# Half of an MLP's second matmul by seven block products instead of eight, with weight sums made by accumulating DMA

## The chip, the cores and the metric

One core of one Trainium2 chip runs the whole program. The metric is the device time of one execution in microseconds (us); lower is better. Five engines work side by side, each with its own in-order queue: TensorE (PE, its weight loads as PEld), VectorE (DVE), ScalarE (ACT), GpSimd (POOL) and SyncE (SP). SP, ACT and POOL also start DMA transfers.

## The reference, cut to what matters

The program is one decoder layer on 256 tokens of width 2048 (three token mixers, their merge, an output projection), then a squared-ReLU MLP and a last norm. The change lies in the last two lines, with `w_mlp_in` 2048 x 8192 and `w_mlp_out` 8192 x 2048, all in float32:

```python
h = h + mixed @ w_out[l]
u = rmsnorm(h, ln2_w[l])
h = h + jnp.square(jax.nn.relu(u @ w_mlp_in[l])) @ w_mlp_out[l]
return rmsnorm(h, lnf_w)[:, CHUNK:]
```

## The kernel before, in words

All weights lie in DRAM as **pieces** of 128 x 1024 float32 (512 KB): eight 128 x 128 blocks along the contraction, for 128 output channels. `weights` (L219) loads a piece into a `raw` buffer by a DMA from SP (L228), then `split` (L200) makes two float32r tiles of it: ACT casts it to `wh` (L201) and DVE subtracts to get the rest, `wl` (L202). So a product of float32 accuracy is made from float32r matmuls: high x high, high x low and low x high.

`product2` (L249) makes one output tile, 128 channels x 256 tokens with a contraction of 2048, from two pieces. The weights are the stationary operand. For each of 16 blocks there is one matmul with `wh` over 512 moving columns (the 256 tokens' high part beside their low part, L257) and one with `wl` over 256 columns (the high part alone, L259).

The MLP runs in four quarters `qd` of the hidden width. A quarter has 16 *mi* tiles (first matmul; ReLU, square and split into `hx`, L1290 to L1298) and then 16 *mo* tiles (second matmul over that quarter's 2048 hidden channels, summed over the quarters in `macc`, L1299 to L1318). Each tile takes two pieces, 256 pieces in all.

What sets the order: the kernel is written as a plain sequence, and a scheduler at build time lays it out on the queues by priority. Loads and splits of pieces are marked `tc.high_priority()`, so that they go as far ahead as their buffers let them. Those buffers are three `wh`, three `wl`, and the `raw` buffers of two pools: `more_raw` holds `(wp, 3)` and, from L1279 on, `(wp2, 3)`, and a counter `n_raw`, raised by one for each piece, sends odd numbers to `wp2` and even numbers to `wp`. A `raw` buffer is free again when both halves of its split are done. The partial sums of *trunk* products lie in three PSUM buffers (`trunk_psum`), others in five (`mx`).

```python
n_raw[0] += 1
rpool, bufs = more_raw[n_raw[0] % len(more_raw)]
raw = rpool.tile([P, 8, P], F32, tag="raw", bufs=bufs, name=uname("raw"))
nc.sync.dma_start(raw, a["w"][first + k])
```

Of the kernel before, what the change touches and what calls it, by code (L numbers as in the profile page):

```python
# [10 lines left out]
F32 = mybir.dt.float32  # L11
# [139 lines left out]
def tile_hybrid(ctx: ExitStack, tc: tile.TileContext, a, out, dbg=None):  # L151
# [23 lines left out]
    def V(k, j=0, n=1, rows=slice(0, P)):  # L175
        return vecs[rows, VCOL[k] + j:VCOL[k] + j + n]
# [13 lines left out]
    def uname(s):  # L190
        cnt[0] += 1
        return f"{s}_{cnt[0]}"
# [26 lines left out]
    def weights(key, ahead=True):  # L219

        first, n = PIECE[key]
        parts = []
        for k in range(n):
            with tc.high_priority() if ahead else ExitStack():
                n_raw[0] += 1
                rpool, bufs = more_raw[n_raw[0] % len(more_raw)]
                raw = rpool.tile([P, 8, P], F32, tag="raw", bufs=bufs, name=uname("raw"))
                nc.sync.dma_start(raw, a["w"][first + k])  # L228
                wh = wp.tile([P, 8, P], F32R, tag="wh", bufs=3, name=uname("wh"))
                wl = wp.tile([P, 8, P], F32R, tag="wl", bufs=3, name=uname("wl"))  # L230
                split(wh, wl, raw)
            parts.append((wh, wl))
        return parts

    def product(key, hi, lo, tok, kts=KT, ahead=True):

        n = tok.stop - tok.start
        ps = trunk_psum(n)
        last = kts // 8 - 1
        for k, (wh, wl) in enumerate(weights(key, ahead)):  # L240
# [8 lines left out]
    def product2(key, x):  # L249
# [11 lines left out]
        return full[:, :NR], full[:, NR:]  # L261

    def sigmoid(dst, src, nbias=0.0, sign=1.0):

# [980 lines left out]
    st_e = ExitStack()  # L1245
    ep = pool(st_e, "ep")
    wp2 = pool(st_e, "wp2")
    h1 = ep.tile([P, 16, NR], F32, name="h1")
    z2 = ep.tile([P, 2, 16, NR], F32R, name="z2")
    acc2 = ep.tile([P, NR], F32, name="acc2")  # L1250
    r2 = ep.tile([P, NR], F32, name="r2")
    macc = ep.tile([P, 16, NR], F32, name="macc")
# [9 lines left out]
    def add_square(c, src):  # L1262
        s = et("sqe")
        act.activation(s, src, AF.Square)
        if c == 0:
            vec.tensor_copy(acc2, s)
        else:
            vec.tensor_tensor(acc2, acc2, s, add)

    for c in range(16):  # L1270
        xr = et("xr", 3)
        nc.scalar.dma_start(xr, a["xt"][:, c, NM:])
        ps, lo = product2(("out", c), m2)
        vec.tensor_tensor(h1[:, c], lo, xr, add)
        vec.tensor_tensor(h1[:, c], ps, h1[:, c], add)
        z = et("z")
        act.activation(z, h1[:, c], AF.Copy, scale=V("ln2", c))
        split(z2[:, 0, c], z2[:, 1, c], z)
        add_square(c, h1[:, c])  # L1279
# [6 lines left out]
    act.activation(r2, r2, AF.Exp, scale=-1.0)  # L1286
    st_y = ExitStack()
    yp = pool(st_y, "yp", side="right")
    for qd in range(4):
        hx = yp.tile([P, 2, 16, NR], F32R, tag="hx", bufs=2, name=uname("hx"))  # L1290
        for c in range(16):
            ps, lo = product2(("mi", 16 * qd + c), z2)
            vec.tensor_tensor(ps, ps, low_part(lo), add)
            r = et("rl")
            act.activation(r, ps, AF.Relu)
# [3 lines left out]
        for c in range(16):  # L1299
            ps, lo = product2(("mo", qd, c), hx)  # L1300
            if qd == 0:
                act.copy(macc[:, c], ps)
            elif qd < 3:
                vec.tensor_tensor(macc[:, c], ps, macc[:, c], add)
            if qd < 3:
                vec.tensor_tensor(macc[:, c], lo, macc[:, c], add)
            else:
                vec.tensor_tensor(ps, ps, low_part(lo), add)
            if qd == 2:
                vec.tensor_tensor(macc[:, c], macc[:, c], r2, mult)  # L1310
                vec.tensor_tensor(h1[:, c], h1[:, c], macc[:, c], add)
            if qd == 3:
                t = et("rs")
                vec.tensor_tensor(t, ps, r2, mult)
                vec.tensor_tensor(h1[:, c], h1[:, c], t, add)
                if c < 15:
                    add_square(c, h1[:, c])
                    act.activation(h1[:, c], h1[:, c], AF.Copy, scale=V("lnf", c))  # L1318
    pn = mx()[:, :NR]
    pe.matmul(pn, lhsT=C("ones"), rhs=acc2, start=True, stop=False)  # L1320
    s = et("sqe")
# [7 lines left out]
    act.activation(rp_, rl, AF.Exp, scale=-0.5)  # L1329
    act.activation(rf, rl, AF.Exp, scale=-0.5)  # L1330
    for k, (lo, hi) in enumerate(((0, 2), (2, 5), (5, 8), (8, 11), (11, 13))):
        vec.tensor_tensor(macc[:, lo:hi], h1[:, lo:hi],
                          rp_.unsqueeze(1).to_broadcast([P, hi - lo, NR]), mult)
        (nc.scalar if k % 2 else nc.sync).dma_start(out[:, lo:hi], macc[:, lo:hi])
    for c in range(13, 16):
        nc.gpsimd.tensor_tensor(macc[:, c], h1[:, c], rf, mult)  # L1336
    nc.scalar.dma_start(out[:, 13:16], macc[:, 13:16])
    st_y.close()
    st_e.close()

# [95 lines left out]
```

## Time and profile before

| | us |
|---|---|
| median of three runs (lowest, highest) | 1904.9 (1904.66, 1906.49) |
| the profiled execution | 1904.59 |
| its span in the trace | 1902.8 |
| PE busy | 1881.6 |
| DVE busy | 1288.1 |
| ACT busy | 1071.3 |
| POOL busy | 189.7 |

The span is the stretch that the trace covers; about 1.8 us of the profiled execution lie around it. A busy share is a mean over the span, so what a stage costs is read from that stage. The granted clock of TensorE has two levels, 1.2 and 2.4 GHz; a value of 1.00 is the upper one.

### The profile page before, as it was taken

Reading aid. Unit: us, or ns where it says so; the run is one execution under the profiler, and the core shown is the slowest. Engines: PE = TensorE matmul, PEld = TensorE weight load, DVE = VectorE, ACT = ScalarE, POOL = GpSimd, SP = SyncE. Lnnn points to the kernel's source line nnn. Section 1 sums busy time; section 2 is a strip of 40 time slices with the busy share of each in tenths; the row PEclk is TensorE's granted clock in tenths of the full one; section 3 lists DMA queues with packets and bytes.
Section 4 is the critical chain, followed back from the end, with each engine's and each line's share of the span. In section 5 each row is a group of like instructions: output and inputs, shape, how many; then the busy total and the mean of one; then the engine's idle time right before and its main releaser. Section 6 shows DMA issues by size and latency. Waiting matters only on the chain.

```text
span 1902.8 us, 35349 instructions
## 1 busy us (share of the span) xinstructions
PE 1881.6 (99%) x13910; PEld 1745.0 (92%) x13910; DVE 1288.1 (68%) x2126; ACT 1071.3 (56%) x1943; POOL 189.7 (10%) x317
## 2 busy tenths in 40 slices
PE   8999999999999999999999999999999999999997
PEld 8999999999999999999999988888888888888886
DVE  7878677668956667677677776654566556775575
ACT  7666566656556667676564455544454345435554
POOL 5110111112111111112121000000000000000000
PEclk9999999999999999999999999999999999999998
DMA  7556544444554445444657775556555555555562
GB/s 248 177 188 197 162 147 156 131 155 163 185 156 155 151 150 194 146 153 161 207 170 220 246 222 194 187 184 187 186 188 187 188 188 187 186 189 183 186 189 99
DMA packets 104103, 340.12 MB, mean 179 GB/s; under 512 B 18216, under 2 KB 21432, under 8 KB 103936
## 3 DMA queue, kind: packets, MB, share of 16 engines
q1 hardware_dynamic: 92480, 316.79, 51.8%
q0 software_dynamic: 8576, 17.67, 3.0%
q10 hardware_dynamic: 2880, 3.39, 0.5%
q8 instruction: 109, 1.79, 0.4%
q14 instruction: 58, 0.48, 0.1%
HBM read 327.72 MB, written 10.08 MB: 178 GB/s over the span
## 4 chain that ended last, share of the span: by engine, by line
PE 97%; DVE 1%; DMA 1%; ACT 0%; issue 0%; SPq 0%; DVEq 0%; POOLq 0%
PE pt L257 28%; PE pt L245 15%; PE pt L243 15%; PE pt L244 15%; PE pt L259 14%; PE px L1090 1%; PE px L628 1%; PE px L741 0%; PE px L723 0%; PE px L778 0%; PE px L635 0%; DMA xt<-in_xt 0%; PE px L644 0%; PE px L555 0%; PE px L352 0%; PE px L707 0%
## 5 line engine op out<-in xcount | busy, mean ns | idle before, releaser
L201 ACT CAST wh<-raw 128x1024 fp32r<-128x1024 f32 (+1 forms) x593 | 620.9, 1047 | 664.5 <-PE pt L244 252.0
L202 DVE TENSOR_TENSOR wl<-raw,wh 128x1024 fp32r<-128x1024 f32 (+1 forms) x593 | 726.0, 1225 | 396.7 <-ACT wh L201 388.8
L245 PE MATMUL pt<-uh,wl 128*128 128x256 f32 (+3 forms) x1984 | 567.5, 286 | 0.0
L243 PE MATMUL pt<-uh,wh 128*128 128x256 f32 (+2 forms) x1984 | 566.5, 286 | 0.0
L244 PE MATMUL pt<-ul,wh 128*128 128x256 f32 (+2 forms) x1984 | 566.3, 285 | 0.0
L245 PEld LDWEIGHTS pt<-uh,wl 128*128 128x128 f32 x1984 | 374.0, 189 | 2.6 <-issue 1.0
L243 PEld LDWEIGHTS pt<-uh,wh 128*128 128x128 f32 x1984 | 374.0, 189 | 2.3 <-issue 0.7
L244 PEld LDWEIGHTS pt<-ul,wh 128*128 128x128 f32 x1984 | 373.4, 188 | 1.8 <-issue 0.3
L257 PE MATMUL pt<-z,wh 128*128 128x512 f32 x1024 | 362.2, 399 | 0.0
L257 PE MATMUL pt<-hx,wh 128*128 128x512 f32 x1024 | 358.9, 393 | 0.0
L259 PE MATMUL pt<-hx,wl 128*128 128x256 f32 x1024 | 287.9, 283 | 0.0
L259 PE MATMUL pt<-z,wl 128*128 128x256 f32 x1024 | 287.4, 281 | 0.0
L257 PEld LDWEIGHTS pt<-z,wh 128*128 128x128 f32 x1024 | 192.4, 188 | 48.0
L257 PEld LDWEIGHTS pt<-hx,wh 128*128 128x128 f32 x1024 | 191.6, 188 | 43.6
L259 PEld LDWEIGHTS pt<-z,wl 128*128 128x128 f32 x1024 | 193.4, 189 | 0.1
L259 PEld LDWEIGHTS pt<-hx,wl 128*128 128x128 f32 x1024 | 192.5, 188 | 0.9
L243 PE MATMUL pt<-oh,wh 128*128 128x256 f32 x384 | 107.9, 281 | 0.0
L244 PE MATMUL pt<-ol,wh 128*128 128x256 f32 x384 | 107.6, 280 | 0.0
L245 PE MATMUL pt<-oh,wl 128*128 128x256 f32 x384 | 107.6, 280 | 0.0
L257 PE MATMUL pt<-m,wh 128*128 128x512 f32 x256 | 89.8, 393 | 0.0
L377 DVE TENSOR_TENSOR pt<-pt,rstd 128x256 f32<-128x256 f32 (+3 forms) x124 | 54.0, 436 | 46.6 <-PE pt L245 46.0
L1336 POOL TENSOR_TENSOR macc<-h,rs 128x256 f32<-128x256 f32 x3 | 2.1, 725 | 826.4 <-ACT rs L1330 826.4
(459 smaller groups left out, 2216.0 us busy)
## 6 DMA issues: line engine op xcount, KB each, us to landing
raw<-in_w SPq DMA_DIRECT2D x591, 512.0 KB, 4.2
rcb<-sc_rc SPq DMA_DIRECT2D x8, 256.0 KB, 3.8
sc_gr<-gt POOLq DMA_DIRECT2D x16, 128.0 KB, 3.6
sc_gm<-gt POOLq DMA_DIRECT2D x16, 128.0 KB, 3.9
sc_gh<-gt POOLq DMA_DIRECT2D x16, 128.0 KB, 3.7
gin<-sc_gr POOLq DMA_DIRECT2D x16, 128.0 KB, 3.4
gin<-sc_gm POOLq DMA_DIRECT2D x16, 128.0 KB, 3.0
gin<-sc_gh POOLq DMA_DIRECT2D x16, 128.0 KB, 3.4
```

Of the source, the lines that this page charges most:

```text
L201: act.copy(dst_h, src)
L202: vec.tensor_tensor(dst_l, src, dst_h.bitcast(F32), sub)
L243: pe.matmul(ps, lhsT=wh[:, j], rhs=hi[:, kt, tok], start=(kt == 0), stop=False)
L244: pe.matmul(ps, lhsT=wh[:, j], rhs=lo[:, kt, tok], start=False, stop=False)
L245: pe.matmul(ps, lhsT=wl[:, j], rhs=hi[:, kt, tok], start=False, stop=(k == last and j == 7))
L257: pe.matmul(full.rearrange("p (a n) -> p a n", a=2), lhsT=wh[:, j], rhs=x[:, :, kt], start=(kt == 0), stop=end, skip_group_check=True)
L259: pe.matmul(full[:, :NR], lhsT=wl[:, j], rhs=x[:, 0, kt], start=False, stop=end, skip_group_check=True)
L377: vec.tensor_tensor(ps, ps, rstd1[:, tok], mult)
L628: ins = pe.matmul(pk[e][:, c], lhsT=kt_[er, t], rhs=ar[er, :, t], start=True, stop=True)
L1090: ins.append(pe.matmul(px[br, 2 * i + c], lhsT=lhs(i, o), rhs=rhs(i, o), start=True, stop=True))
L1336: nc.gpsimd.tensor_tensor(macc[:, c], h1[:, c], rf, mult)
```

## The change: what it does

The second matmul is cut in two. Output tiles 8 to 15 stay as they were. Tiles 0 to 7 (1024 output channels) are computed by a seven-product scheme for 2 x 2 block matrices: tokens in two halves of 128, the quarter's hidden channels in two halves of 1024 (blocks `k`), and the output channels in two halves of 512 (`half`). Here the activations are the stationary operand (`xc`, 128 x 128) and the weights the moving one (512 columns). Products 1, 2 and 5 use two loaded weight blocks and their difference, which DVE makes. Products 3, 4, 6 and 7 use sums of two blocks: SP loads one block and then a DMA from POOL adds the other to the same buffer (`accum_op=add`). The seven operands of activations are made by DVE and ACT in the *mi* tiles 8 to 15. The products are added into `cc_`, and after the last quarter `back` transposes it.

A quarter's seven products are 4 steps of weight 3 (each loads two buffers and makes three splits) and 16 steps of weight 1 (each loads one buffer, adds to it and makes one split); `run` puts them between the pieces of the 8 *mo* tiles of that quarter and the first 8 *mi* tiles of the next one. `wp2` has 2 `raw` buffers instead of 3, `hx` one buffer instead of two. `h1` is no longer kept in SBUF: its tiles are written to DRAM (`sc_h`) and read back by DMAs from ACT.

```diff
+    def raw_tile():
+        n_raw[0] += 1
+        rpool, bufs = more_raw[n_raw[0] % len(more_raw)]
+        return rpool.tile([P, 8, P], F32, tag="raw", bufs=bufs, name=uname("raw"))
+    def parts(raw):
+        wh = wp.tile([P, 8, P], F32R, tag="wh", bufs=3, name=uname("wh"))
+        wl = wp.tile([P, 8, P], F32R, tag="wl", bufs=3, name=uname("wl"))
+        split(wh, wl, raw)
+        return wh, wl
...
-    more_raw.append((wp2, 3))
+    more_raw.append((wp2, 2))
...
-        hx = yp.tile([P, 2, 16, NR], F32R, tag="hx", bufs=2, name=uname("hx"))
+    SEVEN = {1: (0, None, ((0, 1), (3, 1))), 2: (1, None, ((2, 1), (3, -1))),
+             5: (3, None, ((0, -1), (1, 1))), 3: (5, ((0, 1), (1, 1)), ((1, 1), (3, 1))),
+             4: (6, ((1, 0), (0, 0)), ((0, 1), (2, 1))), 6: (2, ((0, 0), (0, 1)), ((3, 1),)),
+             7: (4, ((1, 0), (1, 1)), ((0, 1),))}
+    def block(qd, k, half, s):
+        f = PIECE["mo", qd, 4 * half][0] + k
+        return a["w"][f:f + 7:2].rearrange("c p (j m) -> p c j m", j=8)[:, :, 2 * s:2 * s + 2]
+    def seven_part(ps, xc, i, pair, s):
+        wh, wl = (cols4(t) for t in pair)
+        out_ = ps.rearrange("p (c m) -> p c m", c=4)
+        for j in range(2):
+            kt = 2 * s + j
+            for n, (x, w) in enumerate(((0, wh), (0, wl), (1, wh))):
+                pe.matmul(out_, lhsT=xc[:, SEVEN[i][0], x, kt], rhs=w[:, :, j],
+                          start=(kt == 0 and n == 0), stop=(kt == 7 and n == 2))
+    def seven_add(ps, i):
+        for b, sign in SEVEN[i][2]:
+            if b not in begun:
+                begun.add(b)
+                act.activation(cc_[:, b], ps, AF.Copy, scale=float(sign))
+            else:
+                vec.tensor_tensor(cc_[:, b], cc_[:, b], ps, add if sign > 0 else sub)
+    def seven(qd, xc):
+        ps = {}
+        for s in range(4):
+            def step(s=s):
...
+                with tc.high_priority():
+                    r11, r22 = raw_tile(), raw_tile()
+                    nc.sync.dma_start(cols4(r11), block(qd, 0, 0, s))
+                    nc.sync.dma_start(cols4(r22), block(qd, 1, 1, s))
+                    p2 = parts(r11)
+                seven_part(ps[2], xc, 2, p2, s)
+                with tc.high_priority():
+                    p5 = parts(r22)
+                seven_part(ps[5], xc, 5, p5, s)
+                with tc.high_priority():
+                    vec.tensor_tensor(r11, r11, r22, sub)
+                    p1 = parts(r11)
+                seven_part(ps[1], xc, 1, p1, s)
...
+            yield 3, step
+        for i in (3, 4, 6, 7):
+            for s in range(4):
+                def step(i=i, s=s):
...
+                    with tc.high_priority():
+                        raw = raw_tile()
+                        (k0, h0), (k1, h1) = SEVEN[i][1]
+                        nc.sync.dma_start(cols4(raw), block(qd, k0, h0, s))
+                        nc.gpsimd.dma_start(cols4(raw), block(qd, k1, h1, s), accum_op=add)
+                        pair = parts(raw)
+                    seven_part(ps[i], xc, i, pair, s)
+                    if s == 3:
+                        seven_add(ps[i], i)
+                yield 1, step
...
+        sp = ep.tile([P, 4, P], F32, tag="sp", bufs=1, name=uname("sp"))
+        vec.tensor_tensor(flat(sp[:, 2:4]), r, r, mult)
+        split(hx[:, 0, c], hx[:, 1, c], flat(sp[:, 2:4]))
+        vec.tensor_tensor(flat(sp[:, 0:2]), hx[:, 0, j].bitcast(F32), hx[:, 1, j].bitcast(F32), add)
+        ct = ep.tile([P, 5, P], F32, tag="ct", bufs=1, name=uname("ct"))
...
+        vec.tensor_tensor(ct[:, 0:2], sp[:, 0:2], twice(sp[:, 3]), sub)
+        vec.tensor_tensor(ct[:, 2:4], sp[:, 1:3], twice(sp[:, 0]), sub)
+        vec.tensor_tensor(ct[:, 4], sp[:, 2], sp[:, 3], sub)
+        split(xc[:, 0:5, 0, j], xc[:, 0:5, 1, j], ct)
+        act.copy(xc[:, 5, :, j], hx[:, :, j, 0:128].bitcast(F32))
+        act.copy(xc[:, 6, :, j], hx[:, :, c, 128:256].bitcast(F32))
...
+    def back():
+        for c in range(8):
+            h = et("h", 3)
+            nc.scalar.dma_start(h, sc_h[:, c])
+            pt = mx()[:, :NR]
+            for n in range(2):
+                col = slice(128 * (c % 4), 128 * (c % 4) + 128)
+                pe.transpose(pt[:, 128 * n:128 * n + 128], cc_[:, 2 * n + c // 4, col], ident)
+            t = et("rs")
+            vec.tensor_tensor(t, pt, r2, mult)
+            final(c, t, h)
+    def run(tiles, between=(), over=1, then=None):
...
+                while between and done < total * n / over:
+                    w, step = between.pop(0)
+                    done += w
+                    step()
...
+    run(mi_tile(0, c, hx, xc) for c in range(16))
+    for qd in range(3):
+        work = [mo_tile(qd, c, hx) for c in range(8, 16)]
+        hx_, xc_ = hx, xc
+        hx = hx_tile()
+        work += [mi_tile(qd + 1, c, hx, None) for c in range(8)]
+        run(work, seven(qd, xc_), 30)
+        xc = xc_tile()
+        run(mi_tile(qd + 1, c, hx, xc) for c in range(8, 16))
+    run([mo_tile(3, c, hx) for c in range(8, 16)], seven(3, xc), 11, back)
```

In `run`, `n` counts the pieces of the tiles so far, `total` is the weight of all steps (28), and `over` is the number of pieces over which they are spread (30, and 11 in the last quarter).

## Rows read from the trace of the kernel before

**Rows 1.** The page, its busy engines and its chain of waits by engine and line.
```profile
PE 1881.6 (99%) x13910; PEld 1745.0 (92%) x13910; DVE 1288.1 (68%) x2126; ACT 1071.3 (56%) x1943; POOL 189.7 (10%) x317
...
PE 97%; DVE 1%; DMA 1%; ACT 0%; issue 0%; SPq 0%; DVEq 0%; POOLq 0%
```

**Rows 2.** Windows of the MLP: first quarter's mi tiles, then the sum of four windows.
```profile
core 0: us, PE busy (x) PEld busy (x) DVE busy (x) ACT busy (x) POOL busy (x), PEclk, DMA share, GB/s
1166.30:1257.20 90.90, 90.90 (x516) 78.82 (x515) 55.33 (x80) 47.94 (x81) 0.00 (x0) 1.00 0.57 185
...
sum 722.00, PE 722.00 PEld 629.38 DVE 443.36 ACT 344.30 POOL 0.00; mean PE 180.50 PEld 157.35 DVE 110.84 ACT 86.08 POOL 0.00
```

**Rows 3.** Groups by line and shape from 1166 us on: busy us, mean ns | idle before.
```profile
L257 PE MATMUL pt<-z,wh 128*128 128x512 f32 x1024 | 362.2, 399 | 0.0
L257 PE MATMUL pt<-hx,wh 128*128 128x512 f32 x1024 | 358.9, 393 | 0.0
L202 DVE TENSOR_TENSOR wl<-raw,wh 128x1024 fp32r<-128x1024 f32 x255 | 312.4, 1225 | 253.3 <-ACT wh L201 250.9
L201 ACT CAST wh<-raw 128x1024 fp32r<-128x1024 f32 x254 | 266.7, 1050 | 365.3 <-PE pt L257 204.6 <-issue 160.4
L1293 DVE TENSOR_TENSOR pt<-pt,lo 128x256 f32<-128x256 f32 x64 | 27.2, 426 | 0.0
L1297 DVE TENSOR_TENSOR rs<-rl 128x256 f32<-128x256 f32 x64 | 26.8, 419 | 0.0
L202 DVE TENSOR_TENSOR hx<-rs,hx 128x256 fp32r<-128x256 f32 x64 | 26.7, 417 | 1.9 <-ACT hx L201 1.9
L1306 DVE TENSOR_TENSOR macc<-pt,macc 128x256 f32<-128x256 f32 x48 | 20.3, 422 | 1.0
L1332 DVE TENSOR_TENSOR macc<-h,px 128x768 f32<-128x768 f32 x3 | 2.7, 948 | 0.0
L1332 DVE TENSOR_TENSOR macc<-h,px 128x512 f32<-128x512 f32 x2 | 1.4, 686 | 2.6 <-ACT px L1329 2.6
```

**Rows 4.** Timeline of PE inside a mi tile: start us, duration us.
```profile
1780.01 0.40 PE L257 MATMUL pt<-z,wh 128*128 128x512 f32 x1
1780.25 0.28 PE L259 MATMUL pt<-z,wl 128*128 128x256 f32 x1
1780.36 0.40 PE L257 MATMUL pt<-z,wh 128*128 128x512 f32 x1
1780.59 0.28 PE L259 MATMUL pt<-z,wl 128*128 128x256 f32 x1
```

**Rows 5.** Timeline of PE at two transposes in float32: start us, duration us.
```profile
338.80 0.27 PE L651 MATMUL px<-cst,bt 128*128 128x128 f32 x1
338.91 0.27 PE L652 MATMUL px<-cst,kt 128*128 128x128 f32 x1
339.02 0.38 PE L653 MATMUL px<-cst,tkb 128*96 128x128 f32 x2
```

**Rows 6.** Source line L228, the load of a piece, over the whole span.
```profile
L228 SPq DMA_DIRECT2D raw<-in_w x584: 327/328/425, 25.3 to 1865.4; - x195
```

**Rows 7.** The tile raw from 1170 to 1890 us.
```profile
L228 SPq DMA_DIRECT2D raw<-in_w x247: 327/328/328, 1171.8 to 1865.4; - x124
DMA to landing us min/median/max: 3.1/4.3/6.4
```

**Rows 8.** The tile gin: loads of 128 KB from POOL, durations in ns.
```profile
L1198 POOL DMA_DIRECT2D gin<-sc_gr x16: 536/537/553, 719.5 to 919.6; - x16
DMA to landing us min/median/max: 2.2/3.3/4.8
```

**Rows 9.** Windows at the start of the output projection (columns as in rows 2).
```profile
1084.00:1086.00 2.00, 2.00 (x13) 1.76 (x12) 1.29 (x3) 0.76 (x2) 0.00 (x0) 1.00 1.05 409
```

**Rows 10.** DMA queues from 1076 to 1092 us: packets, MB, share of 16 engines.
```profile
q1 hardware_dynamic: 1158, 4.20, 73.0%
q10 hardware_dynamic: 676, 0.62, 11.3%
```

More of the change, by code (lines that the diff above doesn't have):

```diff
@@ L221, in weights @@
         first, n = PIECE[key]
-        parts = []
         for k in range(n):
             with tc.high_priority() if ahead else ExitStack():
-                n_raw[0] += 1
-                rpool, bufs = more_raw[n_raw[0] % len(more_raw)]
-                raw = rpool.tile([P, 8, P], F32, tag="raw", bufs=bufs, name=uname("raw"))
+                raw = raw_tile()
                 nc.sync.dma_start(raw, a["w"][first + k])
[L229 to L233, printed above, removed]
+                pair = parts(raw)
+            yield pair
+    def raw_tile():
[7 more added lines that the diff above has]
+        return wh, wl
     def product(key, hi, lo, tok, kts=KT, ahead=True):
@@ L239, in product @@
         last = kts // 8 - 1
-        for k, (wh, wl) in enumerate(weights(key, ahead)):
+        for k, (wh, wl) in enumerate(list(weights(key, ahead))):
             for j in range(8):
@@ L247, in product, with steps2 @@
         return ps
-    def product2(key, x):
+    def steps2(key, x):
         full = trunk_psum(2 * NR)
@@ L260, in product2 @@
                           skip_group_check=True)
-        return full[:, :NR], full[:, NR:]
+            yield full[:, :NR], full[:, NR:]
+    def product2(key, x):
+        *_, last = steps2(key, x)
+        return last
     def sigmoid(dst, src, nbias=0.0, sign=1.0):
@@ L1260, in low_part, with add_square @@
         return t
-    def add_square(c, src):
-        s = et("sqe")
+    def add_square(first, src):
+        s = et("sqe", 1)
         act.activation(s, src, AF.Square)
-        if c == 0:
+        if first:
             vec.tensor_copy(acc2, s)
@@ L1288, in tile_hybrid @@
     yp = pool(st_y, "yp", side="right")
-    for qd in range(4):
-        hx = yp.tile([P, 2, 16, NR], F32R, tag="hx", bufs=2, name=uname("hx"))
[L1291 to L1295, printed above, removed]
+    SUMS = ("11-22", "21-22", "21-11", "12-11", "12-22", "11", "22")
+    SEVEN = {1: (0, None, ((0, 1), (3, 1))), 2: (1, None, ((2, 1), (3, -1))),
[3 rows of a table added]
@@ new lines, in seven_add @@
+    def seven_add(ps, i):
[9 more added lines that the diff above has]
+            def step(s=s):
+                if s == 0:
+                    ps.update({i: mx() for i in (1, 2, 5)})
+                with tc.high_priority():
[12 more added lines that the diff above has]
+                if s == 3:
+                    for i in (2, 5, 1):
+                        seven_add(ps[i], i)
[3 more added lines that the diff above has]
+                def step(i=i, s=s):
+                    if s == 0:
+                        ps[i] = mx()
+                    with tc.high_priority():
+                        raw = raw_tile()
+                        (k0, h0), (k1, h1) = SEVEN[i][1]
+                        nc.sync.dma_start(cols4(raw), block(qd, k0, h0, s))
+                        nc.gpsimd.dma_start(cols4(raw), block(qd, k1, h1, s), accum_op=add)
+                        pair = parts(raw)
+                    seven_part(ps[i], xc, i, pair, s)
+                    if s == 3:
+                        seven_add(ps[i], i)
+                yield 1, step
@@ L1296, in tile_hybrid, with mi_tile @@
+    def mi_tile(qd, c, hx, xc):
+        for ps, lo in steps2(("mi", 16 * qd + c), z2):
+            yield
+        vec.tensor_tensor(ps, ps, low_part(lo), add)
+        r = et("rl")
+        act.activation(r, ps, AF.Relu)
+        if c < 8:
             s = et("rs")
@@ L1298, in tile_hybrid @@
             split(hx[:, 0, c], hx[:, 1, c], s)
[L1299 to L1318, printed above, removed]
+            return
@@ new lines, in mi_tile, with mo_tile @@
+        vec.tensor_tensor(ct[:, 2:4], sp[:, 1:3], twice(sp[:, 0]), sub)
[3 more added lines that the diff above has]
+        act.copy(xc[:, 6, :, j], hx[:, :, c, 128:256].bitcast(F32))
+    def mo_tile(qd, c, hx):
+        for ps, lo in steps2(("mo", qd, c), hx):
+            yield
+        m = macc[:, c - 8]
+        if qd == 0:
+            act.copy(m, ps)
+        elif qd < 3:
+            vec.tensor_tensor(m, ps, m, add)
+        if qd < 3:
+            vec.tensor_tensor(m, lo, m, add)
+        else:
+            vec.tensor_tensor(ps, ps, low_part(lo), add)
+            t = et("rs")
+            vec.tensor_tensor(t, ps, r2, mult)
+            final(c, t, m)
+        if qd == 2:
+            vec.tensor_tensor(m, m, r2, mult)
+            h = et("h", 3)
+            nc.scalar.dma_start(h, sc_h[:, c])
+            vec.tensor_tensor(m, m, h, add)
@@ new lines, in run @@
+    def run(tiles, between=(), over=1, then=None):
+        between, done, n = list(between), 0, 0
+        total = sum(w for w, _ in between)
+        for tile_ in tiles:
+            alive = True
+            while alive:
+                try:
+                    next(tile_)
+                    n += 1
+                except StopIteration:
+                    alive = False
+                    continue
+                while between and done < total * n / over:
+                    w, step = between.pop(0)
+                    done += w
+                    step()
+                    if not between and then:
+                        then()
@@ L1331, in tile_hybrid @@
     for k, (lo, hi) in enumerate(((0, 2), (2, 5), (5, 8), (8, 11), (11, 13))):
-        vec.tensor_tensor(macc[:, lo:hi], h1[:, lo:hi],
+        vec.tensor_tensor(h1[:, lo:hi], h1[:, lo:hi],
                           rp_.unsqueeze(1).to_broadcast([P, hi - lo, NR]), mult)
-        (nc.scalar if k % 2 else nc.sync).dma_start(out[:, lo:hi], macc[:, lo:hi])
+        (nc.scalar if k % 2 else nc.sync).dma_start(out[:, lo:hi], h1[:, lo:hi])
     for c in range(13, 16):
-        nc.gpsimd.tensor_tensor(macc[:, c], h1[:, c], rf, mult)
-    nc.scalar.dma_start(out[:, 13:16], macc[:, 13:16])
+        nc.gpsimd.tensor_tensor(h1[:, c], h1[:, c], rf, mult)
+    nc.scalar.dma_start(out[:, 13:16], h1[:, 13:16])
     st_y.close()
```

51 lines of the change are left out of this document (40 added, 11 removed).

## The prediction, made before the changed kernel was run

> **What bounds the kernel now.** The page comes first: PE is busy for 99% of the span, and the chain of waits is 97% PE [rows 1]. A share is a mean, so the second view is the windows of the stage that is changed: through the 722.0 us of the MLP, PE is busy for all 722.0, DVE for 443 and ACT for 344, at a granted clock of 1.00, the upper of its two levels, and DMA moves some 185 GB/s [rows 2]. So only matmul columns shorten this stage, and the question is whether anything else becomes late when columns go.
>
> **Matmuls, removed and added.** The MLP has 1024 + 1024 pairs of one 512-column and one 256-column matmul [rows 3]; 722.0 / 2048 = 0.3525 us a pair. Their starts show 0.235 us for the 512 columns and 0.115 for the 256 [rows 4]; weight loads hide at either pace. The 399 ns of one matmul is a modelled, overlapping duration and not a price. Removed are 4 quarters x 8 tiles x 16 pairs = 512 x 0.3525 = 180.5 us. Added are 4 x 7 products x 24 matmuls of 512 columns = 672 x 0.235 = 157.9 us, an eighth less: **-22.6 us**. The sixteen transposes in `back` start 0.11 us apart in the nearest rows [rows 5]: **+1.8 us**. All else has to hide beside PE. If it does, the result is 1904.6 - 20.8 = 1883.8 us (the sum is made against the profiled execution, 1904.6; the median is 0.3 higher).
>
> From here on a piece of an ordinary tile is N (eight pairs, 8 x 0.3525 = 2.82 us of PE) and a step with an accumulating DMA is A (six matmuls, 1.41 us).
>
> **DVE and ACT.** In one mixed stretch (16 ordinary tiles and one quarter's products; 90.2 + 39.5 = 129.7 us of PE) DVE has 60 splits and 4 differences at 1.225 us, up to 12 additions of 512 columns at 0.69, eight mi tiles with three operations of about 0.42 and eight mo tiles with two [rows 3]: 78 + 8 + 10 + 7 = 103 us, 80%. ACT has 60 casts at 1.05 us and some 10 us more. Both fit, at nothing. In the mi tiles 8 to 15 DVE has 2 x 1.225 for splits, 1.26 for what was there, a sum and three differences at no more than 0.42 each, and a split of 640 columns, between the 0.69 of 512 and the 0.95 of 768, so 0.82: 6.2 us in a tile of 5.64 us of PE. The excess, 0.57 x 8 = 4.5 us a quarter, is work that no matmul waits for at once, since the splits have priority and `xc` is read later; I take 0, with 18 us over four quarters as the upper bound and 0 as the lower. The stores and reloads of `h` on ACT's queue (0.33 us to issue by the nearest row, a load from SP [rows 7]) are some three dozen, spread over tiles; I take 0, and a dozen us if each delayed a cast that PE waits for.
>
> **The loads.** This is where I expect the loss. A step A cannot start its second transfer before the first has landed, since both go to the same `raw` buffer. POOL's queue holds nothing else in this stage, and an accumulation waiting there delays only later ones; but SP's queue is in order, and behind a load that waits for its buffer stand the loads of ordinary pieces. A buffer is held for: load, addition, cast, subtraction. The load is 4.3 us (3.1 to 6.4) [rows 7]. The sum's transfer is not in this trace: the nearest POOL loads, 128 KB each, land after 3.3 us (2.2 to 4.8) [rows 8]; 384 KB more at the 409 GB/s of a saturated stretch [rows 9] is 0.96 us: 4.3. Its 1 KB runs cost nothing extra: packets of about 0.9 KB took 0.113 x 16 x 16 us / 676 = 43 ns (21 GB/s an engine), the ones of 3.6 KB 161 ns (23 GB/s) [rows 10]. With 1.05 + 1.23 for the split and 0.2 of handing over (my estimate, four hand-overs of 0.05) the **hold is 11.1 us**. Its bounds: 3.1 + 3.2 + 2.3 = 8.6, and 6.4 + 5.8 + 1.3 (the destination read as well) + 2.3 + 1 (a busy DVE) = 16.8.
>
> Which buffers? 584 pieces are numbered in all [rows 6], 256 of them in the MLP, so the first mi piece is number 329 and goes to `wp2`. Counting on through `run`: after the first 13 pieces and 4 large steps the first two A go to `wp`, then one even count (28 x 15 / 30 = 14, no step) shifts the parity, and the remaining **14 A of each quarter all go to `wp2`, which now has two buffers**, while the pieces N between them use the three of `wp`. A pair of A thus passes every 11.1 us, where the written order wants one N and one A in 4.23, a pair in 8.5.
>
> The buffer of the first of these 14 comes free when N12 starts on PE, plus its split, 2.3 us. Seven holds later, 77.7, the last is split, and 1.4 us of PE follow: 81.4 us. PE's own work from N12 to there is 17 N and 16 A, 70.5 us. Late by **10.9 us a quarter, 33 us in the first three**. If PE takes the three N behind the last A early (8.5 us), 2.4 is left.
>
> In the last quarter the steps lie closer, and A use both pools. From A number 3 to the last, `wp2` carries 7 A and 3 N (hold 6.7): 97.8 / 2 = 48.9 us from half a microsecond before N4 starts, and 1.4 of PE; PE's work is 7 N and 16 A, 42.3. Late by **7.5 us**. The transferred bytes agree: 39 transfers of 0.52 MB at 409 GB/s take 50 us.
>
> **Sum.** -22.6 + 1.8 + 33 + 7.5 = +19.7: **1924 us**. On its own this case spans 1909 to 1945 (hold 10.6 to 11.9).
>
> **Rivals.**
> *The sums arrive in time* (faster). The point is the hold at which nothing is late: (70.5 - 3.7) / 7 = 9.5 us, so load and sum together 7.0 us. Bounds of the two reach down to 6.3, and after fast landings or with N pulled ahead of a late A by the scheduler the loss is 0 to 2.4 a quarter and about 2 to 7 at the end: 1886 to 1898, in the middle 1890. For it: PE's queue is laid out by a scheduler that may put ready work first, and today no cast waits for a load, only for PE or its own queue [rows 3]. Against: the median load alone is 4.3. The Trainium skill, "DMA: Bandwidth & Descriptors", section "Anatomy of one DMA — SWDGE (gpsimd) path", gives some 2.0 us plus bytes / 436 GB/s, for 512 KB an estimate of 3.2 us; by it two transfers would take 6.4 and all would be hidden. The trace's 4.3 us for one such transfer is above it [rows 7].
>
> *The sum reads twice* (slower still). If an accumulating transfer occupies the DMA engines for its destination's bytes too, it takes 1.3 us more (0.52 MB at 409 GB/s): hold 12.4, late by 20 us a quarter and 12 at the end, -20.8 + 60 + 12 = +51: 1956. No row shows an accumulation, for or against; traffic of four units for an N and an A in 4.23 us would be 496 GB/s, over the 409 seen. The Trainium skill, "Collectives: The Full Stack", section "The bandwidth ceiling: the fold count and why AG ≠ RS ≠ AR", says that an add in the DMA needs two source reads and so halves the rate; no run here shows it for a sum into SBUF.
>
> *DVE takes over* (no change). The sums are in time, but the excess of the mi tiles 8 to 15 is not hidden: 1884 + 18 = 1902. Against it: 80% load in the stretch behind, where the backlog can go.
>
> **How the numbers follow.** Forecast 1924: 0.34. Twice read, 1956 and more: 0.18. In time, 1886 to 1898: 0.38, much for a rival, because one unseen duration decides, and two microseconds of hold separate gain and loss. No change, 1902 or the edge between the cases: 0.10. A measurement can tell about 0.2%, 3.8 us, from none. So faster 0.38, same 0.10, slower 0.52. The range runs from 1885 to 1980: the bounds of the hold reach from below 1885 to 2070, and I leave out a tenth at each end. The likeliest case's own range stands above.
>
> **What would show it.** The 512-column matmuls of the products should start 0.235 us apart, 672 of them. If the loads are late, PE has gaps at the A steps from the third A of a quarter on, ended by ACT's cast, which waits for the DMA from POOL; that DMA lands after more than 4 us, and `raw` in `wp2` turns over every 5.5 us. If I am wrong, PE is 99% busy there, and the accumulation lands within 3 us, or other pieces stand in the gaps. Gaps ended by `hx` or `xc` would mean DVE.

## The result, and the profile after

| | before | after |
|---|---|---|
| median (lowest, highest), us | 1904.8 (1904.3, 1906.5) | 2127.4 (2124.4, 2130.0) |
| span of the profiled execution | 1902.8 | 2125.4 |

The ratio is 1.117, 95% interval [1.115, 1.118]: **223 us slower**. The direction was forecast, but 1924 and the range up to 1980 were far too low.

The page of the changed kernel, its engines, its chain by engine and line, and the loads of `raw`:

```profile
PE 1938.8 (91%) x13574; PEld 1758.6 (83%) x13574; DVE 1420.9 (67%) x2330; ACT 1155.4 (54%) x2075; POOL 269.6 (13%) x381
...
PE 74%; DMA 18%; DVE 3%; ACT 3%; issue 2%; SPq 0%; ACTq 0%; POOLq 0%; POOL 0%; DVEq 0%
...
raw<-in_w SPq DMA_DIRECT2D x623, 512.0 KB, 4.2
raw<-in_w POOLq DMA_DIRECT2D x64, 512.0 KB, 8.6
```

Against [rows 1], DMA has risen from 1% of the chain to 18%, all of it `raw<-in_w`. The accumulating transfer, 64 of them, lands after 8.6 us, twice what the forecast took.

Windows by stage, to be read against [rows 2]: the first quarter's mi tiles, the first mixed stretch, the mi tiles 8 to 15 behind it, and all that follows:

```profile
1166.00:1257.00 91.00, 91.00 (x517) 78.93 (x516) 66.23 (x108) 54.84 (x100) 0.00 (x0) 1.00 0.59 190
1257.00:1450.00 193.00, 154.12 (x717) 126.23 (x717) 101.36 (x122) 80.28 (x116) 20.64 (x16) 0.89 0.80 202
1450.00:1500.00 50.00, 49.76 (x280) 42.74 (x279) 46.06 (x81) 33.82 (x60) 0.00 (x0) 1.00 0.57 179
1500.00:2110.00 610.00, 484.87 (x2265) 395.64 (x2263) 363.25 (x516) 254.24 (x366) 61.67 (x48) 0.89 0.76 196
```

Where no products are mixed in, PE is full as before. In the mixed stretch PE idles 39 of 193 us, and its granted clock falls to a mean of 0.89. The forecast had 129.7 us of PE's work in the mixed stretch and 10.9 us of lateness; the window of 193 us also holds some work of the tiles behind it. DVE is busy for 101 of 193 us and is not the bound.

The waits from 1160 us to the end (us in total, times, longest):

```profile
POOL raw L1374 <- DMA raw<-in_w: 535.3, 37, 234.1
...
ACT wh L201 <- DMA raw<-in_w: 291.2, 43, 10.3
...
PE px L1330 <- ACT wh L201: 149.4, 35, 9.1
```

PE waits for ACT's cast, and the cast waits for a DMA, which it never did before [rows 3]. Source line L1374, the accumulation, and L1373, the load ahead of it, each from issue to landing:

```profile
L1374 POOL DMA_DIRECT2D raw<-in_w x64: 1273/1282/1361, 1302.2 to 2079.9; - x64
...
DMA to landing us min/median/max: 5.5/8.6/12.7
```

```profile
L1373 SPq DMA_DIRECT2D raw<-in_w x64: 367/378/385, 1295.1 to 2074.4; - x64
...
DMA to landing us min/median/max: 3.5/5.2/10.1
```

The chain of waits around 1362 us, in order of time (start, us, what), shows one turn of a buffer:

```profile
1353.28 9.07 DMA raw<-in_w
...
1362.45 1.05 ACT wh L201
...
1363.52 1.24 DVE wl L202
...
1364.78 4.65 DMA raw<-in_w
...
1369.45 0.04 POOLq L1374
1369.50 0.48 issue
...
1369.99 8.31 DMA raw<-in_w
...
1378.40 1.05 ACT wh L201
```

From cast to cast are 15.95 us: 1.05 for the cast, 1.24 for the subtraction, 4.65 for the load, 8.31 for the sum and 0.7 for handing over, most of it on POOL's queue. This turn repeats, and each one carries two N and two A, so a pair takes 8.0 us where PE needs 4.23. The third accumulation of the quarter, the first of the 14 in `wp2`, and its sixteenth start at:

```profile
1320.55 1.27 POOL L1374 DMA_DIRECT2D raw<-in_w  x1 [14.82 <-DMA raw<-in_w]
```

```profile
1423.21 1.28 POOL L1374 DMA_DIRECT2D raw<-in_w  x1 [3.37 <-DMA raw<-in_w]
```

These are 13 steps in 102.7 us, 7.9 us each: two buffers of `wp2`, each held for about 16 us. The load at 1364.78 starts 0.02 us behind the end of a split, so it waited for that buffer.

The timeline of PE at the end of one such gap, and windows of 2 us around it (PEclk is the third number from the end):

```profile
1363.54 0.79 PE L1330 MATMUL px<-wh,xc 128*128 128x512 f32 x1 [5.04 <-ACT wh L201]
...
1367.86 0.41 PE L265 MATMUL pt<-z,wl 128*128 128x256 f32 x1
1368.07 0.63 PE L263 MATMUL pt<-z,wh 128*128 128x512 f32 x1
1368.50 0.41 PE L265 MATMUL pt<-z,wl 128*128 128x256 f32 x1
...
1370.48 0.40 PE L263 MATMUL pt<-z,wh 128*128 128x512 f32 x1
1370.72 0.28 PE L265 MATMUL pt<-z,wl 128*128 128x256 f32 x1
1370.84 0.39 PE L1330 MATMUL px<-wh,xc 128*128 128x512 f32 x1
```

```profile
1364.00:1366.00 2.00, 1.85 (x5) 1.29 (x5) 2.00 (x3) 0.71 (x2) 0.00 (x0) 0.50 0.27 51
1366.00:1368.00 2.00, 2.00 (x7) 1.61 (x6) 1.04 (x3) 1.74 (x3) 0.00 (x0) 0.50 0.89 229
...
1370.00:1372.00 2.00, 2.00 (x12) 1.68 (x11) 0.31 (x1) 0.00 (x0) 1.27 (x1) 1.00 1.32 262
```

After 5.04 us of idleness the granted clock is 0.50, the lower level, and a 512-column matmul starts 0.43 us before the next one; some six microseconds later it is back at 1.00 and 0.24. So the work behind a gap takes longer too; what that is worth in the kernel's time is asked of e9 below.

### The profile page after: what moved, and what is told of

Same layout as the page of the kernel before. It is cut to its first block, busy times and chain, and to the rows that moved or that the text cites. A ratio compares the mean times of both kernels' runs of the same rounds, so it can differ in the third digit from the quotient of the medians.

```text
span 2125.4 us, 35388 instructions
## 1 busy us (share of the span) xinstructions
PE 1938.8 (91%) x13574; PEld 1758.6 (83%) x13574; DVE 1420.9 (67%) x2330; ACT 1155.4 (54%) x2075; POOL 269.6 (13%) x381
## 4 chain that ended last, share of the span: by engine, by line
PE 74%; DMA 18%; DVE 3%; ACT 3%; issue 2%; SPq 0%; ACTq 0%; POOLq 0%; POOL 0%; DVEq 0%
DMA raw<-in_w 18%; PE pt L263 14%; PE pt L250 14%; PE pt L248 14%; PE pt L249 14%; PE pt L265 7%; PE px L1330 3%; ACT wh L201 2%; DVE wl L202 2%; PE px L1100 1%; PE px L638 1%; PE px L751 0%; PE px L645 0%; PE px L733 0%; PE px L654 0%
## 5 line engine op out<-in xcount | busy, mean ns | idle before, releaser
L202 DVE TENSOR_TENSOR wl<-raw,wh 128x1024 fp32r<-128x1024 f32 (+1 forms) x641 | 778.4, 1224 | 467.7 <-ACT wh L201 458.5
L201 ACT CAST wh<-raw 128x1024 fp32r<-128x1024 f32 (+1 forms) x641 | 666.5, 1049 | 764.8 <-DMA raw<-in_w 293.3
L263 PE MATMUL pt<-z,wh 128*128 128x512 f32 x1024 | 383.4, 414 | 4.3 <-ACT wh L201 4.3
L1330 PE MATMUL px<-wh,xc 128*128 128x512 f32 x448 | 182.7, 463 | 149.4 <-ACT wh L201 149.4
L1330 PEld LDWEIGHTS px<-wh,xc 128*128 128x128 f32 x448 | 99.4, 222 | 181.1 <-ACT wh L201 161.8
L1374 POOL DMA_DIRECT2D raw<-in_w x64 | 82.3, 1286 | 930.7 <-DMA raw<-in_w 535.3
L263 PE MATMUL pt<-hx,wh 128*128 128x512 f32 x512 | 189.8, 406 | 5.7 <-ACT wh L201 5.7
L265 PE MATMUL pt<-hx,wl 128*128 128x256 f32 x512 | 146.1, 288 | 0.9 <-DVE wl L202 0.9
L263 PEld LDWEIGHTS pt<-hx,wh 128*128 128x128 f32 x512 | 99.4, 194 | 31.6 <-ACT wh L201 9.4
L1330 PE MATMUL px<-wl,xc 128*128 128x512 f32 x224 | 103.2, 461 | 2.6 <-DVE wl L202 2.5
```

The source lines that it names most:

```text
L1330: pe.matmul(out_, lhsT=xc[:, SEVEN[i][0], x, kt], rhs=w[:, :, j], start=(kt == 0 and n == 0), stop=(kt == 7 and n == 2))
L1374: nc.gpsimd.dma_start(cols4(raw), block(qd, k1, h1, s), accum_op=add)
```

## The experiments

The runs up to e15 were made once each, e16 to e19 four times. Four runs of the changed kernel lie within 5.6 us, four of e17 within 12.6, so differences of a few us between single runs say nothing.

**The accumulation taken away, or made plain.** e1 drops it, so products 3, 4, 6 and 7 use one block each; e2 lets the second transfer overwrite.

```diff
-  nc.gpsimd.dma_start(cols4(raw), block(qd, k1, h1, s), accum_op=add)     # e1
+  nc.gpsimd.dma_start(cols4(raw), block(qd, k1, h1, s))                   # e2
```

> Leaves out the accumulating transfer of the products 3, 4, 6 and 7 (their weights are one block instead of a sum of two); all else is as in the changed kernel. Theory 1 (chain: one raw buffer is held for a load, then an accumulation of 8.6 us, then a split, 16 us in all, and 14 of 16 such steps of a quarter share two buffers): the hold falls to some 7 us, nothing is late, 1884 to 1900 us. Rival A (the accumulating packets fill the DMA engines, whatever the buffers): also 1884 to 1900. Rival B (other parts of the change cost it: DVE in the mi tiles 8 to 15, the stores and reloads of h on ACT's queue, SP's order): stays above 1950 us.

> The second transfer from POOL stays, into the same buffer and behind the first, but overwrites instead of adding (the weights of products 3, 4, 6 and 7 are the second block alone). Theory 1 (chain): a plain second transfer lands after some 5 us instead of 8.6, the hold is 13 instead of 16, a pair of steps every 13 us instead of 16.2: some 20 us a quarter less than the changed kernel, about 2040 us. Rival A (DMA engines full because adding packets take 101 ns instead of 43): three plain transfers take 3.9 us of the 4.23 of a piece and a step, so nothing is late: 1884 to 1920 us.

Measured 1905.5 and 2065.0. The whole loss against the kernel before is the second transfer: 159.5 us for waiting on any second transfer, and another 62.4 us because it accumulates (in packets of 1 KB, where the plain one moves 3.6 KB, see e5). In e2, theory 1 was 25 us too low, and rival A as the whole cause is refuted. In e1 1905.5 lies 5 us above the range of theory 1 and far below rival B.

**The pool.** e3 sends the steps A to `wp` and `wp2` in turn; e8 does so with e2's plain transfer.

```diff
+        rpool, bufs = more_raw[turn.pop() if turn else n_raw[0] % len(more_raw)]
...
+                        turn.append(s % 2)
                         raw = raw_tile()
```

> The accumulating steps take the two raw pools in turn instead of 14 of 16 from the one with two buffers; the transfers are the same. Theory 1 (chain over two buffers): the three-buffer pool carries two pieces and one step in 30 us / 3, the other one step in 8 us, so a piece and a step pass every 5.0 us instead of 8.1, late by 13 us a quarter and as much at the end: about 1950 us. Rival A (DMA engines full): an accumulation takes 512 packets x 101 ns / 16 = 3.2 us and two loads 1.3 each, 5.8 us a piece and step, late by 25 us a quarter: about 1985 us, with a DMA share near 1. If neither buffers nor engines matter: 2127 us.

> As the run with the plain second transfer (2065 us), and with the steps taking the two pools in turn. Theory 1 (chain of landings over too few buffers, where the DMA engines have room): a step holds its buffer 14 us and a piece 7, 21 us over five buffers is 4.2 us for a piece and a step: little is late, 1920 to 1980 us. Theory 2 (with accumulation the spread over pools did nothing, so the buffers were not the limit there or anywhere; the order of the queues is): 2050 to 2080 us again.

Measured 2128.5 and 2062.6: nothing, in either pair, so theory 1 missed both times. What fails is its premise that a piece N gives up its buffer after 7 us. That two buffers of `wp2` hold up the A is what the changed kernel shows, 7.9 us a step; one ring of all five buffers would give 15.95 / 2.5 = 6.4. In e2 the same 13 steps take 92.3 us, 7.1 each, and its hold is 5.3 + 6.0 + 3.0 = 14.3, twice that. In e3 half of the A go to `wp`, whose three buffers then carry three of every four items, and the 13 steps take 103.4 us, again 8.0 each: the shortage moved along with the A. No run has five buffers in one ring, so that the count goes by pools rests on these paces. Theory 2 of e8 has the right number here; e11 below refutes its cause, the order of the queues.

**PE's own work doubled.** e9 does the matmuls of products 3, 4, 6 and 7 twice, 384 x 0.235 = 90 us more of PE.

```diff
-            for n, (x, w) in enumerate(((0, wh), (0, wl), (1, wh))):
+            for n, (x, w) in enumerate(((0, wh), (0, wl), (1, wh)) * times):
```

> The changed kernel with each matmul of the products 3, 4, 6 and 7 done twice (these products come out doubled): 384 more matmuls of 512 columns, 90 us at full clock. Theory 1 (the stretch is set by load, sum and split, and PE waits): the time stays within 20 us of 2127, and may fall where the clock is kept up. Rival D (PE at a lower clock is what sets the time): 90 to 150 us longer, 2215 to 2280 us.

Measured 2122.7, within a few us of the time without them, as theory 1 has it; the mean granted clock of the span is 0.974 against 0.955. In the mixed stretches PE's work is free, and the lower clock behind the gaps is not what sets the time.

**Longer runs.** In e5 both transfers read whole pieces in 4 KB runs (other blocks than the scheme wants).

```diff
+                        f = PIECE["mo", qd, 4 * h0][0] + k0 + 2 * s
+                        nc.sync.dma_start(raw, a["w"][f])
+                        nc.gpsimd.dma_start(raw, a["w"][f + 1 - 2 * k0], accum_op=add)
```

> Both transfers of a step read whole pieces in runs of 4 KB instead of 1 KB (so the sums are of other blocks than they should be). Theory 1 with the add itself as the price (each destination byte is read too): the accumulation still lands after 7 us or more, 2080 to 2127 us. Rival E (the price is the 512 short packets: 1.28 us of POOL for 512 descriptors, 101 ns a packet): POOL takes 0.55 us, the landing falls to some 5 us, 1990 to 2040 us.

Measured 2093.6, in the range of theory 1; an accumulation still lands after 7.7 us at the median. The queue of the accumulations from 1310 to 1410 us (packets, MB, share of 16 engines) in the changed kernel, in e2 and in e5:

```profile
q0 software_dynamic: 6438, 6.39, 40.8%
```

```profile
q0 software_dynamic: 1871, 6.81, 19.5%
```

```profile
q0 software_dynamic: 1770, 6.40, 36.0%
```

A packet takes share x 16 x 100 us / packets: accumulating, 101 ns per 1 KB and 325 ns per 3.6 KB; plain, 167 ns per 3.6 KB, as in [rows 10] (161), which also has 43 ns for 0.9 KB. So **an accumulation occupies the DMA engines about twice as long at equal packets**, and in 1 KB runs 528 packets x 101 ns / 16 = 3.3 us for each 512 KB.

**DVE makes the sum, with five and with six buffers.** e4 loads both blocks from SP into two buffers; e7 frees room for a sixth buffer by single buffers elsewhere.

```diff
-                        raw = raw_tile()
+                        raw, other = raw_tile(), raw_tile()
...
+                        nc.sync.dma_start(cols4(other), block(qd, k1, h1, s))
+                        vec.tensor_tensor(raw, raw, other, add)
...
+    more_raw.append((wp2, 3))   # e7 alone
```

> Both blocks of a sum are loaded by SP into two raw buffers and DVE adds them (1.22 us); no accumulating transfer. The same bytes are read from DRAM. Theory 1: no second landing behind a first; a step holds its buffers 9 and 6.5 us, a piece 7.6, 23 us over five buffers is 4.6 us for a piece and a step against 4.23 of PE: late by 6 us a quarter, about 1905 to 1925 us. Rival A in the form that traffic from DRAM is the limit: no better than the changed kernel, above 2000 us. Rival C (DVE becomes the bound: 103 + 20 us in a stretch of 130, above 130 with the backlog of the tiles before): 1930 to 1960 us, with DVE ending the gaps.

> As the sum on DVE (2059 us), with six raw buffers instead of five (room from single buffers for lo, rl and rs, two for h). Theory 1 (the buffers are too few for the landings): 6.4 us for a piece and a step fall by a sixth to 5.3, some 65 us less: about 1990 us. If DVE or the queue order is the limit: 2040 to 2060 us.

Measured 2059.4 and 1964.0. One more `raw` buffer is worth 95 us, although e7 gave up buffers of other tiles for it; a step takes 5.2 us instead of 6.6 in the first quarter. Since the sixth buffer went to `wp2`, the smaller pool, e7 doesn't tell one ring from two. In e4 only rival A has the right number, but e12 below moves the same bytes in 1945.7, so traffic from DRAM is not the limit at 2059.

**Nine buffers.** Operands 5 and 6 of `xc` are copies of parts of `hx`; the products can read `hx` itself, which makes room for six `wp2` buffers.

```diff
-    more_raw.append((wp2, 2))
+    more_raw.extend([(wp2, 6)] * 2)
...
+        return hx[:, x, kt, 0:128] if m == 5 else hx[:, x, 8 + kt, 128:256]
```

The second transfer is accumulating (e10), plain (e11), from SP with DVE's sum (e12), left out (e13), or from SP with POOL's sum (e14).

> The changed kernel with nine raw buffers instead of five, used by all pieces and steps in turn; the room comes from products 3 and 4, which read hx itself instead of a copy of it. Theory 3 (pieces and steps are used in order, so all raw buffers go round together once per load, sum and split of 16 us; five of them hold 2 to 2.5 pairs of a piece and a step, 6.4 to 8 us a pair against 4.23 of PE): nine hold 4.5 pairs, 3.6 us a pair, and nothing is late on that account: 1890 to 1915 us. Rival A (an accumulation fills the DMA engines for 3.2 us, each load for 1.3: 5.8 us a pair whatever the buffers): 64 x 1.6 = 100 us stay: 1985 to 2020 us with a DMA share near 1.

> Nine raw buffers, and the second transfer overwrites instead of adding (the weights of products 3, 4, 6 and 7 are the second block alone). Theory 3: 14 us / 4.5 = 3.1 us a pair, the engines need 3.9: nothing is late, 1888 to 1910 us. If the queue order itself is the limit (theory 2): still above 2000 us, as with five buffers.

> Nine raw buffers, two loads by SP and the sum on DVE; the output is complete. Theory 3: three buffers a pair, three pairs in 11 us, 3.7 us a pair: 1890 to 1920 us. Rival C (DVE, with 123 us of work in a stretch of 130, becomes the bound): 1925 to 1950 us, gaps ended by DVE.

> Nine raw buffers and no second transfer (the weights of products 3, 4, 6 and 7 are one block instead of a sum of two): the floor of the scheme. Theory 3: what was left in the run without the second transfer (1905 against 1884 by matmuls alone) was also short buffers, in the last quarter: 1886 to 1895 us. Rival: DVE at the end and the longer tail keep it at 1898 to 1906 us.

> Nine raw buffers, two loads by SP and the sum on POOL instead of DVE; the output is complete. If the DVE's extra work made the run with the sum on DVE 1946 us (rival C), POOL, which is idle here, takes it away: a sum of 1024 columns is 4 x 0.73 = 2.9 us there, 16 of them 47 us in a stretch of 130: 1900 to 1915 us, as with the plain second transfer (1905). If the 512 KB more per step from DRAM and their place in SP's queue made it, 1935 to 1950 us stay.

| second transfer | five buffers | nine buffers |
|---|---|---|
| none | 1905.5 | 1896.0 |
| plain | 2065.0 | 1904.9 |
| accumulating | 2127.4 | 1982.2 |
| sum on DVE | 2059.4 | 1945.7 |
| sum on POOL | - | 1974.7 |

With nine buffers the waiting for a second transfer is hidden (8.9 us left of 159.5), and what remains depends on who adds. Theory 3 of e11 and rival C of e12 came true; e10 is 3 us below its rival A, e13 lies between its two ranges, and e14 is above both of its own. In e10 the DMA engines are full; the window from 1320 to 1390 us and its queues:

```profile
1320.00:1390.00 70.00, 59.28 (x290) 45.84 (x288) 36.79 (x46) 27.97 (x39) 15.42 (x12) 1.00 1.14 284
```

```profile
q0 software_dynamic: 6571, 6.53, 57.9%
q1 hardware_dynamic: 7720, 13.31, 56.3%
```

The share stands at 1.14 at only 284 GB/s, where [rows 9] had 409 GB/s; twelve accumulations in 70 us are 5.8 us a pair against PE's 4.23. In e12 DVE has 64 sums of 1.22 us more, 78 us, and is busy for 621 of 739 us from 1166 us on:

```profile
1166.00:1905.00 739.00, 700.12 (x3647) 583.32 (x3645) 620.64 (x848) 396.13 (x551) 0.00 (x0) 0.99 0.74 245
```

The surprise is e14, whose sums leave DVE: its splits, in e12 and in e14 (ns, min/median/max), and a stretch of both engines in e14:

```profile
L202 DVE TENSOR_TENSOR wl<-raw,wh x296: 1211/1219/1228, 1165.3 to 1903.9; 128x1024 fp32r<-128x1024 f32 x148
```

```profile
L202 DVE TENSOR_TENSOR wl<-raw,wh x287: 1206/1225/3432, 1167.3 to 1900.8; 128x1024 fp32r<-128x1024 f32 x144
...
1341.27 2.35 POOL L1380 TENSOR_TENSOR raw<-raw,raw 128x1024 f32<-128x1024 f32 x1 [0.43 <-DMA raw<-in_w]
...
1341.95 2.76 DVE L202 TENSOR_TENSOR wl<-raw,wh 128x1024 fp32r<-128x1024 f32 x1 [4.97 <-ACT wh L201]
```

A split that meets a sum on POOL lasts until some 1.1 us after POOL's end, as if it did its work behind it. All 40 splits that start during a sum end 1.08 to 1.10 us behind it; the 74 that overlap one take 2.13 us at the mean, the 229 others 1.22.

**Spreading the steps.** In the changed kernel the four large steps come first and the sixteen A densely behind them. e15 is e10 with one large step and then four A, four times; e16 (POOL's sums) and e17 (accumulating) also compute the last quarter with eight products, which gives up a quarter of the gain.

```diff
+            between = [x for k in range(4) for x in between[k:k + 1] + between[4 + 4 * k:8 + 4 * k]]
...
-    run([mo_tile(3, c, hx) for c in range(8, 16)], seven(3, xc), 11, back)
+    run(mo_tile(3, c, hx) for c in range(16))
```

> Nine raw buffers and accumulating transfers as in the run of 1982 us, but the 16 accumulating steps of a quarter are spread over the whole stretch (each large step, then four of them) instead of its second half; all transfers are the same, the output is complete. If an accumulation occupies the DMA engines for 3.2 us and a load for 1.3: 2 pieces, one such step and a quarter of a large one need 7.7 us of the engines and 8.1 of PE, so in the first three quarters nearly all of the 78 us that lie between 1982 and 1905 go, less in the last, where the steps lie twice as close: 1915 to 1940 us. If an accumulation is late for its own latency, wherever it stands: 1970 to 1990 us again.

> Nine raw buffers, sums on POOL, the steps spread over the whole stretch, and the last quarter with eight products as in the kernel before (the transposes are added to its tiles in PSUM). The output is complete. By matmuls alone: 3 x 5.65 less, 1.8 more, 1889.5 us; with some us of short waits 1890 to 1900 us, below the kernel before. If POOL's sums slow DVE or come late: 1905 to 1930 us.

> As the run before, with accumulating transfers from POOL in place of loads and sums on POOL. The output is complete. If the DMA engines' time is all that an accumulation costs (7.7 us of 8.1): 1890 to 1905 us; if it also delays the loads around it: 1910 to 1940 us.

Measured 1943.0; 1952.0 (ratio 1.024 [1.023, 1.026]); 1928.2 (1.012 [1.009, 1.015]). Spreading gives the accumulations back 39 us: from 1320 to 1390 us there are 8 of them instead of 12, the DMA share is 0.98 instead of 1.14, and PE is busy for 66.0 us instead of 59.3. POOL's sums gain nothing by it: a quarter's products take 137 to 142 us in e16 and 134 to 135 in e14. e15 is 3 us above its first range, e16 22 above its second, and e17 lies in its second. e17 is the fastest of all that make the sums, and it loses 1.2% to the kernel before.

**The rest.** Is what e17 still loses the adder's load again? e18 puts the sums on DVE, e19 two of each four.

```diff
+                        if s % 2:     # e19; e18 always
+                            other = raw_tile()
+                            nc.sync.dma_start(cols4(other), block(qd, k1, h1, s))
+                            vec.tensor_tensor(raw, raw, other, add)
```

> Nine buffers, steps spread evenly, last quarter with eight products, as in e17, but the other block is loaded by SP and DVE makes the sum (as in e12). Theory 1 (with nine buffers the loss is the resource that makes the sum: the DMA engines at 100 ns per 1 KB packet for the accumulation, DVE for its sums; what is spread evenly loses less): DVE has some 16 x 1.2 = 19 us more in a mixed stretch of 130 us, 122 us of 130, with peaks still above; between e17 and e12 without its last quarter, 1910 to 1935. Rival (the loss in the first halves of the stretches has another cause than either resource, such as the parity of the buffers or ACT): as e17, 1920 to 1933 whoever makes the sum, and e19 the same.

> As e17 and e18, but two of each product's four sums by accumulating DMA and two by DVE. Theory 1 (two resources, each overloaded only when it makes all the sums): both carry half, so that less is lost than in e17 and in e18: 1895 to 1912, the floor being 1889.5 by matmuls (1904.6 less three quarters of 20.8) plus the 12 us that e13 lost with no sums at all in part. Rival (another cause): the mean of e17 and e18 or above.

Measured 1968.4 (1.034 [1.032, 1.035]) and 1947.3 (1.023 [1.021, 1.025]). e19 is the mean of the other two (1948.3): the rival's number, a miss for my theory; e18 is above both of its ranges. Two windows of e19:

```profile
1340.00:1350.00 10.00, 10.00 (x55) 8.49 (x54) 7.43 (x10) 5.42 (x8) 0.00 (x0) 1.00 1.11 328
...
1360.00:1370.00 10.00, 8.61 (x42) 6.61 (x41) 10.00 (x14) 4.54 (x6) 1.28 (x1) 1.00 0.92 234
```

From 1290 to 1360 us PE is full in every window of 10 us, where e17 loses 3 us and e18 some 9; in this stretch, that part was the adder's. But at 1360 us DVE is busy throughout (its timeline there has seven additions to `cc` between splits and sums), and PE loses 5 us in the 30 from 1360 on. Even spreading brings the ends of four products together. e18 is even slower than e12, which has more sums on DVE and no spreading. Whether those bursts are the whole of it **stays open**; no run separates them.

## Why the prediction was right and wrong

*Matmuls, -22.6 us: right as far as it can be seen.* 672 matmuls of 512 columns are there, 0.23 to 0.24 us apart at full clock. With nothing to wait for (e13) the kernel takes 1896.0, 12 us above the 1883.8 that the sum gives without loads. PE is busy for 192.7 of the 193 us from 1257 us on there; the 12 us lie later, mostly in the last quarter and the tail, and were not taken apart.

*DVE and ACT at 0: right for the kernel as changed.* In the window with the mi tiles 8 to 15 DVE is busy for 46.06 of 50 us, less than the 6.2 in 5.64 that were counted, and PE for 49.76. The rival "DVE takes over" came true only where DVE was given the sums (e12).

*The loads: the right wait, and a hold that was sized too small.* The failed step is "the **hold is 11.1 us**". Its largest term, the landing of the sum, was taken as 4.3 us, with 5.8 + 1.3 as the upper bound; it is 8.6 at the median, and the load ahead of it takes 5.2 instead of 4.3. The hold is 16 us, within the bounds of 8.6 to 16.8, but the forecast stood near their lower end. What hangs on it came as described: gaps at the A, ended by ACT's cast, which waits for POOL's DMA, and two A in each turn of `wp2`, one every 7.9 us instead of 5.5. By the forecast's own formula 16 us would give 2.3 + 7 x 16 + 1.4 - 70.5 = 45 us a quarter, and about 2045 in all. Measured against e13, the first quarter's products take 175.7 us (1261.5 to 1437.2) instead of 118.4, the next two are late by 58 and 60 us: of the first 57 us, 50 are lost from the third A to the sixteenth and 7 before, where the forecast has nothing.

A second step failed in the last quarter, "3 N (hold 6.7)". ACT casts the pieces in order, so an N behind an A waits with its buffer full: the one loaded at 1365.91 landed after 4.8 us, and ACT casts no piece from 1368.5 until the A at 1378.40. That row is from the first quarter. In the last one N and A share both pools, and the products take 129.8 us instead of e13's 70.9, 59 us late instead of 7.5; the formula with 16 us for A and 6.7 for N gives 25. How those buffers turn was not followed, so what of the 2127 lies above 2045 is located, 12 to 15 us in each of the first three quarters, 34 in the last and the 12 of e13, but its cause **stays open**. The clock, which no row of before could price, cost little (e9).

*"The sum reads twice": right in mechanism, too small.* It was given 1956 by adding 1.3 us to the hold. The packets show the factor: 325 against 161 to 167 ns at 3.6 KB. The Trainium skill, "Collectives: The Full Stack", section "The bandwidth ceiling: the fold count and why AG ≠ RS ≠ AR", has it for the reductions of collectives that an add in the DMA needs two source reads; the factor of about 2 agrees with that, though no row shows the reads themselves. At 1 KB runs it is 101 / 43 = 2.3. What I left out is that this is engine time as well as latency: 16 x 3.3 us a quarter, on engines that the loads of N and A also use, which alone keeps the dense order from its pace when buffers are no limit (e10 against e11, 77 us).

*"In time": refuted by a wide margin.* It needed load and sum in 7.0 us; they take 13. The Trainium skill's "DMA: Bandwidth & Descriptors", section "Anatomy of one DMA — SWDGE (gpsimd) path", makes an estimate of 3.2 us for 512 KB issued by GpSimd. The prediction held it against a load from SP [rows 7]; the plain transfer of e2 is issued by GpSimd, and beside the other traffic it takes nearly twice the estimate:

```profile
L1374 POOL DMA_DIRECT2D raw<-in_w x64: 748/748/766, 1302.8 to 2020.0; - x64
...
DMA to landing us min/median/max: 3.9/6.0/8.4
```

## What to carry to other kernels

Where transfers and casts are consumed in order, each pool of prefetch buffers is a ring, as far as the paces here show, and the slowest one sets the pace of all: the time per item is the hold (load + sum + split) divided by the pool's buffers, here 15.95 / 2 = 8.0 us for an A, with 7.9 measured. Count that before counting matmuls, with every item held as long as the slowest ahead of it, and bound the one duration that no trace has yet shown by a run of its own. Price an accumulating DMA twice, in latency and in the DMA engines' time (share x 16 x window / packets), and see whether the mixed stretch has that time free. Test an idea's ceiling first by leaving the added work out: here it was 1896 us, 9 us of gain, far less than any way of making the sums costs.

## What was not expected of the hardware

- POOL is busy for 1.28 us to issue an accumulation of 512 KB in 1 KB runs; in 4 KB runs it takes 0.87 us (e5), without the addition 0.75 (e2), and the loads of [rows 8] 0.54.
- The plain second transfer of the same blocks moves in packets of 3.6 KB (6.81 MB / 1871), the accumulating one in packets of 1 KB.
- With nine buffers an accumulation lands after 11.3 us at the median and up to 16.3 (e10), although a pair then passes faster; the DMA engines are full there.
- POOL's sum of 128 x 1024 takes 2.75 us at the mean (e14), more than twice DVE's 1.22, and holds DVE up besides. The Trainium skill, "SBUF — State Buffer", section "🔬 SBUF: two separate sides", describes an exclusive lock between the two for operations with two SBUF inputs; the 2.76 us split beside the POOL sum agrees, as do the 40 that end 1.08 to 1.10 us behind one.
